# Second product of an MLP on one core: matrix rows change at a time of their own for each product, operands loaded a unit ahead in three buffers, sums on DVE

## The chip, the core and the metric

The kernel runs on one core of a Trainium2 chip. The time is that of the whole program on the device, in microseconds (us). Engines are named as in the profile: PE is TensorE (PEld its weight loads), DVE is VectorE, ACT is ScalarE, POOL is GpSimd, SP is the engine whose queue issues the DMAs.

## What is computed

A diffusion block in fp32: adaLN modulation, a mixer (a Hyena long convolution beside gated linear attention), and an MLP with a squared ReLU. The change lies in the MLP; the mixer, which takes the first half of the time, is untouched.

```python
x  = x + g1 * (mixer(...) @ w_out)
h2 = rms_norm(x, norm_mlp) * (1 + sc2) + sh2          # (2048, 1024)
x  = x + g2 * (square(relu(h2 @ w_mlp1)) @ w_mlp2)    # w_mlp1 (1024, 4096), w_mlp2 (4096, 1024)
return rms_norm(x, norm_final)
```

## The kernel before

**Arithmetic.** Every fp32 matrix product is made of three matmuls: an operand is split into a high part (a cast to fp32r by ACT, line 231 or 1570) and a low part (the rest, by DVE at 232, or by POOL at 1571), and hi x hi, hi x lo and lo x hi are summed in PSUM. On top of that both products of the MLP use a scheme of seven block products in place of eight for a 2 x 2 block product: sums and differences of blocks of either operand are formed ahead, seven products numbered 1 to 7 are taken in the order 1, 2, 6, 5, 7, 4, 3 (`ORDER`), and their results go into the four output blocks. `PR` says which combination of either operand a product reads.

**First product** (lines 1465 to 1547). For two halves of the rows (`tb`), 16 units; each holds seven products of twelve matmuls (four slices `kp`, three each, line 1374). `fill_split` makes the seven combinations of the moving operand resident in `bh`, `bl` for each `kp`; `put` squares the results and stores the seven combinations that the second product needs in DRAM, in `d_m`, by `store`. Products 4 and 3 of a unit (`late4`, `late3`) are issued within the next unit.

**Second product** (lines 1554 to 1677). 64 units: `at = 8 g + t`, t one of eight blocks of 256 output rows, g one of eight pairs of 256-row slices of `w_mlp2` (`kb` = 0, 1). A unit's product is six matmuls (`full2`: two `kb`, three each) into one PSUM bank of 128 x 512, and `more` (line 1600) adds that bank by DVE to the output block `acc` in SBUF; seven sums a unit. The PSUM bank of a unit goes on collecting, so the next product on it waits until the sum before has read it.

**What has to be ready for a unit.** (a) The operand `ur`, seven combinations of 128 x 256, loaded from `d_m` by SP (`load_u`, line 1565, two DMAs), in two buffers; per product ACT makes `uh` and POOL `ul` (`split_u`), in one tile each, so that ACT waits for the product that reads the old one. (b) The matrix rows: `w2_raw` loads a 1 MB row slice, POOL multiplies it by the gate `g2b` (four operations, line 1449) and makes two differences (1452, 1453); `w2_split` makes `wh` and `wl` for a product, and `sum_b` on POOL (1245, 1247) two more differences. Of the two `kb` slices one is replaced every four units: both `kb` have a period of eight units, four apart, for all products at the same unit boundary:

```python
    def rows(at):
        return 2 * (at // 8), 2 * ((at + 4) // 8 % 8) + 1
```

The refill of a product is issued right behind that product of the unit before (4 and 3: within the unit itself), so five splits of a change fall into one unit and two into the next. The gates of a slice are issued in two lots of two, half-way through a unit.

**Order.** Each engine, and the DMA queue of SP, works in the order of issue; what waits holds up all behind it on the same engine. Every tile is released to its next use by semaphores; the order above is written by hand.

**Ends.** `acc` is 16 tiles in a pool of its own, loaded from `d_x1` in the first eight units just before use. In the last eight units, ACT squares the block of the unit before (`squares`), POOL makes the reciprocal root, and DVE scales a row tile of 128 x 1024 (`finish`, line 1624), which SP stores.

Of the kernel before, what the change touches and what calls it, by code (L numbers as in the profile page):

```python
# [210 lines left out]
def hybrid_block(ctx: ExitStack, tc, a, out, dbg=None):  # L211
# [18 lines left out]
    def split(hi, lo, src):  # L230
        nc.scalar.copy(hi, src)  # L231
        dve.tensor_sub(lo, src, hi.bitcast(F32))  # L232
# [15 lines left out]
    d_g2 = dr.tile([P, D], F32, name="d_g2")  # L248
# [969 lines left out]
    e2 = ctx.enter_context(ExitStack())  # L1218
    bp = [sb("bp0", stack=e2), bq, bq]
# [28 lines left out]

    def fill_split(kp, r):
        pool = bp[kp]  # L1250
        hi = pool.tile([P, 7, 512], F32R, tag=f"bh{kp}", bufs=1, name="bh")
        lo = pool.tile([P, 7, 512], F32R, tag=f"bl{kp}", bufs=1, name="bl")
        for m in ORDER:
            j = PR[m][1]
            split(hi[:, j, :], lo[:, j, :], r[:, PLACE[j], :])
            sum_b(r, m, dve)
        bops[kp] = (hi, lo)
# [20 lines left out]
    with ExitStack() as eo:  # L1278
# [80 lines left out]
        ew.close()  # L1359
    e3 = ctx.enter_context(ExitStack())  # L1360
# [5 lines left out]
    g2b = us.tile([P, D], F32, name="g2b")  # L1366

    def prod(ps, w, m, kp, start, stop):
        hi, lo = w[m]
        bh, bl = bops[kp]  # L1370
        j = PR[m][1]
        sl = slice(kp * P, (kp + 1) * P)
        for i, (x_, y_) in enumerate(((hi, bh), (hi, bl), (lo, bh))):
            mm(ps[:], x_[:, sl], y_[:, j, :], start=start and i == 0, stop=stop and i == 2, skip_group_check=True)  # L1374

    def full(ps, w, m, start):
        for kp in range(4):
            prod(ps, w, m, kp, start and kp == 0, kp == 3)
# [8 lines left out]
    def put(n, tb, i, j, src, add=None):  # L1387

        tag, bufs = ("c0", 2) if i == j == 0 else ("c1", 2) if i == j else ("c", 5)
        c = us.tile([P, 512], F32, tag=tag, bufs=bufs, name="c")  # L1390
        if add is None:
            act(c[:], src[:], AF.Relu)
        else:
            dve.tensor_add(c[:], src[:], add[:])
            act(c[:], c[:], AF.Relu)
        act(c[:], c[:], AF.Square)
        cs_[n, i, j] = c
        if (i, j) != (0, 1):
# [5 lines left out]
        eng.tensor_tensor(s1[:], c[:], cs_[n, 1, 1][:], op=ALU.add)  # L1404
        eng.tensor_sub(s2[:], s1[:], cs_[n, 0, 0][:])
        dve.tensor_sub(c[:], cs_[n, 0, 0][:], c[:])
        dve.tensor_sub(s4[:], cs_[n, 1, 0][:], s2[:])
        for slot, t in ((3, c), (4, s1), (5, s2), (6, s4)):
            store(n, tb, slot, t)

    def store(n, tb, slot, c):
        step = lambda: dma(d_m[tb, n, :, :, slot, :], c[:].rearrange("p (q t) -> p q t", q=4))
        if held is None:
            step()
        else:
            held.append(step)
# [26 lines left out]
    def w2_raw(n):  # L1443

        r = w2r[n] = raw_tile()
        dma(r[:, 0:4, :], a["w2"][n])
        yield
        for q in range(4):
            gps.tensor_mul(r[:, q, :], r[:, q, :], g2b[:, (q // 2) * 512:(q // 2 + 1) * 512])  # L1449
            if q == 1:  # L1450
                yield
        gps.tensor_sub(r[:, 4, :], r[:, 3, :], r[:, 0, :])
        gps.tensor_sub(r[:, 3, :], r[:, 2, :], r[:, 3, :])

    def w2_split(n, m):
        kb = n % 2
        r, j, k = w2r[n], PR[m][1], PR[m][0]
        pool, th, tl = (mf, f"vh{k}", f"vl{k}") if kb else (wm, f"wh{k}", f"wl{k}")
        hi = pool.tile([P, 512], F32R, tag=th, bufs=1, name="wh")
        lo = pool.tile([P, 512], F32R, tag=tl, bufs=1, name="wl")  # L1460
        split(hi[:], lo[:], r[:, PLACE[j], :])
        sum_b(r, m, gps)
        w2s[m, kb] = (hi, lo)
# [3 lines left out]
    for tb in range(2):  # L1467
# [8 lines left out]
        for at in range(1, 16):  # L1476
# [5 lines left out]
            if at < 15:  # L1482
                rn = rw[ns[at + 1]] = w_raw(ns[at + 1])
            elif tb == 0:
                raws.append(fill_raw(1, 0, gps))
            else:
                for _ in w2_raw(0):
                    pass
            if at == 2 and tb == 0:
                gate_rows(g2b, us, 24, "p1")  # L1490
                dma(d_g2[:], g2b[:])
# [5 lines left out]
            if late:  # L1497
                late[0]()
# [8 lines left out]
            if late:  # L1507
                late[1]()
            if at > 1:
                w[3] = w_split(r, 3)  # L1510
            if at == 15 and tb == 0:
                raws.append(fill_raw(1, 1, gps))
            elif at == 15:
                for _ in w2_raw(1):
                    pass
# [16 lines left out]
            def late4(n=n, x=x, w=w, tb=tb):  # L1532
                full(x, w, 4, False)
                put(n, tb, 1, 0, x)

            def late3(n=n, y=y, w=w, u2=u2, tb=tb):
                full(y, w, 3, False)
                put(n, tb, 0, 1, y, u2)
# [4 lines left out]
        if tb:  # L1543

            held = []
        late[0]()
        late[1]()
    e3.close()
    eq.close()
# [4 lines left out]
    uu = sb("uu", side="right", stack=em)  # L1554
    uts, ops = {}, {}
    NU = 64

    def rows(at):
        return 2 * (at // 8), 2 * ((at + 4) // 8 % 8) + 1

    def load_u(at):
        t = at % 8
        uts[at] = uu.tile([P, 2, 7, P], F32, tag="ur", bufs=2, name="ur")
        for kb, n in enumerate(rows(at)):
            dma(uts[at][:, kb], d_m[t // 4, n, :, t % 4])

    def split_u(at, m):
        hi, lo = (uu.tile([P, 2, P], F32R, tag=f"{t}{m}", bufs=1, name=t) for t in ("uh", "ul"))
        src = uts[at][:, :, PR[m][0], :]
        nc.scalar.copy(hi[:], src)  # L1570
        (gps if at else dve).tensor_sub(lo[:], src, hi[:].bitcast(F32))  # L1571
        ops[at, m] = (hi, lo)

    load_u(0)
    load_u(1)
    for step in held:
        step()
    e2.close()
    mf = sb("mf", stack=em)
    for m in ORDER[:5]:  # L1580
        split_u(0, m)
        w2_split(1, m)
    acc = [mf.tile([P, D], F32, name=f"acc{t}") for t in range(16)]
    nf = mf.tile([P, D], F32, name="nf")
    dma(nf[:], a["norm_final"].partition_broadcast(P))
    g2b = mf.tile([P, D], F32, name="g2b")
    dma(g2b[:], d_g2[:])
# [9 lines left out]
    def more(ps, t, i, j):  # L1597

        ac = acc[2 * t + i][:, j * 512:(j + 1) * 512]
        dve.tensor_add(ac, ac, ps[:])  # L1600
# [9 lines left out]
    def squares(t):  # L1610
        rs_ = []
        for i in range(2):
            ss = mf.tile([P, 4], F32, tag="ss", bufs=4, name="ss")
            for j in range(2):
                tmp = mf.tile([P, 512], F32, tag="tmp", bufs=4, name="tmp")
                act(tmp[:], acc[2 * t + i][:, j * 512:(j + 1) * 512], AF.Square, accum_out=ss[:, j:j + 1])
            gps.tensor_add(ss[:, 2:3], ss[:, 0:1], ss[:, 1:2])
            rs_.append(rstd_of(mf, ss[:, 2:3], 1, 1.0 / D, "mrs"))
        return rs_

    def finish(t, rs_):
        for i in range(2):
            x2, tile = acc[2 * t + i], 2 * t + i
            dve.scalar_tensor_tensor(x2[:], x2[:], rs_[i][:], nf[:], op0=ALU.mult, op1=ALU.mult)
            dma(out[tile * P:(tile + 1) * P, :], x2[:])

    late = None
    prep = iter(())
    for at in range(NU):
        g, t = divmod(at, 8)  # L1630
        if g == 0:
            for i in range(2):
                dma(acc[2 * t + i][:], d_x1[(2 * t + i) * P:(2 * t + i + 1) * P, :])
# [10 lines left out]
        refill(at, 4)  # L1644
        full2(x, at, 6, False)
        more(x, t, 0, 1)
        refill(at + 1, 6)
        if late:
# [10 lines left out]
        refill(at + 1, 5)  # L1659
        full2(x, at, 7, False)  # L1660
        more(x, t, 1, 1)
        refill(at + 1, 7)
        if rs_:
            finish(t - 1, rs_)
# [9 lines left out]
        late = (late4, late3)  # L1674
    late[0]()
    late[1]()
    finish(7, squares(7))


# [16 lines left out]
```

## Time and profile before

| what | us |
|---|---|
| median of three runs (lowest, highest) | 2703.89 (2701.45, 2707.12) |
| the profiled execution, its own time | 2693.43 |
| its span, first to last instruction | 2691.6 |
| PE busy in the span | 2501.2 (93%) |
| DVE busy | 1573.9 (58%) |
| POOL busy | 1165.4 (43%) |
| ACT busy | 1162.6 (43%) |
| second product, first to last matmul | 1956.3 to 2681.5 |

Busy time of PE is modelled from the start and size of each matmul and overlaps with its neighbours: a matmul of 128 x 512 is shown with 0.39 us, while they start 0.23 us apart when nothing is in their way. So stalls of PE are read from the number of matmuls in a stretch of time, not from its busy share. In a row of waits the columns are the total, the number of times and the longest; in a row of the windows view, each engine has its busy time with the number of instructions in brackets, then come the granted clock of PE, the busy share of the DMA engines and what they moved in GB/s; in a row of an operation by tile, its number, its shortest, median and longest duration in ns, and the first and last start. In the timeline and in the chain, a row begins with its start and its duration.

### The profile page before, as it was taken

What the parts mean: (1) busy time and instruction counts of PE and PEld (TensorE: products, weight loads), DVE (VectorE), ACT (ScalarE), POOL (GpSimd) and SP (SyncE); (2) the same over time, 40 slices, a digit from 0 to 9 for tenths busy, and PEclk for the clock granted to TensorE, in tenths of its full rate; (3) what the DMA queues carried; (4) which work ended last, traced back from release to release, by engine and by line L of the source; (5) the groups of instructions that cost most, each with busy time, mean ns of one, the idle gap of its engine ahead of it and who ended that gap; (6) DMA issues with size and microseconds to landing.
All of it is one profiled execution on the core that took longest, in us unless ns stands there. A gap on an engine that the chain in (4) does not pass through costs nothing.

```text
span 2691.6 us, 38121 instructions
## 1 busy us (share of the span) xinstructions
PE 2501.2 (93%) x13320; PEld 2061.2 (77%) x13320; DVE 1573.9 (58%) x2530; ACT 1162.6 (43%) x2270; POOL 1165.4 (43%) x1155
## 2 busy tenths in 40 slices
PE   9798999999998789899999998999989898989887
PEld 5678978898887778688778886888867677777765
DVE  5754366735567777734555557555564555555557
ACT  6464352225225556334555555555532323232334
POOL 2130231214112223233244444444677776777677
PEclk9899999999999899899999999999999998999999
DMA  5425444433547786556445555454573333333333
GB/s 194 145 80 175 122 134 141 136 113 99 173 149 198 216 249 188 188 188 216 144 148 157 152 149 169 149 159 150 153 277 124 102 108 105 108 104 108 110 105 149
DMA packets 300143, 406.08 MB, mean 151 GB/s; under 512 B 24740, under 2 KB 224296, under 8 KB 289712
## 3 DMA queue, kind: packets, MB, share of 16 engines
q1 hardware_dynamic: 297072, 395.27, 46.5%
q10 hardware_dynamic: 2880, 8.39, 0.8%
q8 instruction: 105, 1.72, 0.3%
q14 instruction: 86, 0.70, 0.1%
HBM read 272.97 MB, written 130.62 MB: 150 GB/s over the span
## 4 chain that ended last, share of the span: by engine, by line
PE 40%; POOL 5%; DMA 5%; DVE 4%; issue 3%; ACT 2%; SPq 0%; POOLq 0%; ACTq 0%; DVEq 0%
PE ps L1374 21%; PE ps L1594 13%; DMA ur<-d_m 3%; POOL ul L1571 3%; PE po L227 2%; PE po L228 2%; PE po L226 2%; POOL raw L1449 1%; DVE wl L232 1%; DVE bl L232 1%; DMA raw<-in_w_dram 1%; DMA raw<-in_w_out_dram 1%; DVE acc L1600 1%; ACT wh L231 1%; ACT uh L1570 1%
## 5 line engine op out<-in xcount | busy, mean ns | idle before, releaser
L232 DVE TENSOR_TENSOR wl<-raw,wh 128x512 fp32r<-128x512 f32 x336 | 342.3, 1031 | 202.5 <-ACT wh L231 201.8
L1571 POOL TENSOR_TENSOR ul<-ur,uh 128x256 fp32r<-128x256 f32 x441 | 362.4, 848 | 168.8 <-ACT uh L1570 151.0
L1594 PE MATMUL ps<-wh,uh 128*128 128x512 f32 x896 | 363.2, 406 | 66.6 <-DVE acc L1600 44.0
L1600 DVE TENSOR_TENSOR acc<-acc,ps 128x512 f32<-128x512 f32 x448 | 300.5, 683 | 185.8 <-PE ps L1594 181.7
L1594 PE MATMUL ps<-wh,ul 128*128 128x512 f32 x896 | 360.5, 403 | 11.8 <-POOL ul L1571 11.5
L1594 PE MATMUL ps<-wl,uh 128*128 128x512 f32 x896 | 359.8, 402 | 0.0
L1570 ACT CAST uh<-ur 128x256 fp32r<-128x256 f32 x448 | 161.5, 403 | 453.9 <-DMA ur<-d_m 301.0
L1374 PE MATMUL ps<-bh,wh 128*128 128x512 f32 x896 | 350.6, 393 | 6.8 <-ACT bh L231 2.4
L1374 PE MATMUL ps<-bh,wl 128*128 128x512 f32 x896 | 350.4, 392 | 3.2 <-DVE wl L232 3.2
L1374 PE MATMUL ps<-bl,wh 128*128 128x512 f32 x896 | 351.0, 392 | 2.6 <-DVE bl L232 2.5
L231 ACT CAST wh<-raw 128x512 fp32r<-128x512 f32 x336 | 207.0, 620 | 207.5 <-PE ps L1374 168.2
L1594 PEld LDWEIGHTS ps<-wh,uh 128*128 128x128 f32 x896 | 175.0, 195 | 117.8 <-ACT uh L1570 57.0
L1594 PEld LDWEIGHTS ps<-wh,ul 128*128 128x128 f32 x896 | 174.5, 195 | 56.6 <-POOL ul L1571 19.2
L1374 PEld LDWEIGHTS ps<-bh,wh 128*128 128x128 f32 x896 | 169.3, 189 | 46.5 <-ACT bh L231 4.0
L1594 PEld LDWEIGHTS ps<-wl,uh 128*128 128x128 f32 x896 | 174.9, 195 | 36.3
L1374 PEld LDWEIGHTS ps<-bl,wh 128*128 128x128 f32 x896 | 169.2, 189 | 39.7 <-DVE bl L232 4.6
L1374 PEld LDWEIGHTS ps<-bh,wl 128*128 128x128 f32 x896 | 169.0, 189 | 39.0 <-DVE wl L232 4.0
L226 PE MATMUL ph<-hth,whi 128*128 128x512 f32 x384 | 150.9, 393 | 0.0
L226 PE MATMUL pv<-whi,hth 128*128 128x264 f32 x512 | 147.4, 288 | 3.2 <-ACT whi L231 2.9
L228 PE MATMUL ph<-hth,wlo 128*128 128x512 f32 x384 | 149.6, 390 | 0.4 <-DVE wlo L232 0.4
L227 PE MATMUL ph<-htl,whi 128*128 128x512 f32 x384 | 149.4, 389 | 0.0
L228 PE MATMUL pv<-whi,htl 128*128 128x264 f32 x512 | 145.5, 285 | 0.4 <-DVE htl L348 0.4
(284 smaller groups left out, 5047.9 us busy)
## 6 DMA issues: line engine op xcount, KB each, us to landing
ur<-d_m SPq DMA_DIRECT2D x128, 448.0 KB, 3.6
raw<-in_w_dram SPq DMA_DIRECT2D x48, 1024.0 KB, 6.3
d_m<-c SPq DMA_DIRECT2D x128, 256.0 KB, 2.6
d_m<-s SPq DMA_DIRECT2D x96, 256.0 KB, 3.3
xt<-in_x_dram SPq DMA_DIRECT2D x32, 512.0 KB, 4.4
mwt<-in_wada_dram SPq DMA_DIRECT2D x64, 256.0 KB, 3.0
raw<-in_wi_vg_dram SPq DMA_DIRECT2D x20, 528.0 KB, 4.7
wada<-in_wada_dram SPq DMA_DIRECT2D x16, 512.0 KB, 7.3
```

The source lines that it names most:

```text
L226: mm(ps, lh, rh, start=first, stop=False)
L227: mm(ps, lh, rl, start=False, stop=False)
L228: mm(ps, ll, rh, start=False, stop=last)
L231: nc.scalar.copy(hi, src)
L232: dve.tensor_sub(lo, src, hi.bitcast(F32))
L1374: mm(ps[:], x_[:, sl], y_[:, j, :], start=start and i == 0, stop=stop and i == 2, skip_group_check=True)
L1449: gps.tensor_mul(r[:, q, :], r[:, q, :], g2b[:, (q // 2) * 512:(q // 2 + 1) * 512])
L1570: nc.scalar.copy(hi[:], src)
L1571: (gps if at else dve).tensor_sub(lo[:], src, hi[:].bitcast(F32))
L1594: mm(ps[:], x_[:, kb, :], y_[:], start=start and kb + i == 0, stop=kb == 1 and i == 2, skip_group_check=True)
L1600: dve.tensor_add(ac, ac, ps[:])
```

## The change

- Each product has its own time for a new row slice (`CHANGE`): 1, 2 and 6 change one unit earlier than 5, 7, 4 and 3, whose change stays; `load_u` then takes two DMAs for a slice that straddles.
- `ur` has three buffers, loaded three units ahead (two before); `uh` and `ul` have two tiles for each product.
- The differences of the matrix rows (`sum_b` in the second product, and two in `w2_raw`) go from POOL to DVE. The four gates stay on POOL, issued one at a time, each between two refills (`slot`).
- In a refill the operand's copies are issued ahead of the matrix's.
- The turn: the resident operand of slices 0 and 3 is cut into tiles of 128 x 512, the last two products of the first stage read slice 0 last, their `put`s move behind the first loads and splits of the second product, and all four combinations of the last unit are made on POOL. `acc` now lies in the space of the resident operand of slices 1 and 2, loaded in pairs of tiles.
- The gate rows `g2b` stay in SBUF, where they went through DRAM.
- Squares and the final scaling are cut into halves of a row tile, the scaling issued one half at a time between products; of the last block, three of four squares are issued ahead of the last product. The guard `at + 4 < NU` around `w2_raw` is gone.

```diff
-    bp = [sb("bp0", stack=e2), bq, bq]
+    bp = [sb("bp0", stack=em), bq, bq]
...
+    def part(kp, h, j):
+        return bp[kp].tile([P, 512], F32R, tag=f"b{h}{kp}_{j}", bufs=1, name=f"b{h}")
...
+    g2b = sb("gp", stack=em).tile([P, D], F32, name="g2b")
...
-        eng = dve if tb and n < 1 else gps
-        eng.tensor_tensor(s1[:], c[:], cs_[n, 1, 1][:], op=ALU.add)
-        eng.tensor_sub(s2[:], s1[:], cs_[n, 0, 0][:])
-        dve.tensor_sub(c[:], cs_[n, 0, 0][:], c[:])
-        dve.tensor_sub(s4[:], cs_[n, 1, 0][:], s2[:])
+        eng = dve if held is None else gps
+        gps.tensor_tensor(s1[:], c[:], cs_[n, 1, 1][:], op=ALU.add)
+        gps.tensor_sub(s2[:], s1[:], cs_[n, 0, 0][:])
+        eng.tensor_sub(c[:], cs_[n, 0, 0][:], c[:])
+        eng.tensor_sub(s4[:], cs_[n, 1, 0][:], s2[:])
...
-    def w2_raw(n):
+    def w2_raw(n, engs):
 
         r = w2r[n] = raw_tile()
         dma(r[:, 0:4, :], a["w2"][n])
-        yield
-        for q in range(4):
-            gps.tensor_mul(r[:, q, :], r[:, q, :], g2b[:, (q // 2) * 512:(q // 2 + 1) * 512])
-            if q == 1:
-                yield
-        gps.tensor_sub(r[:, 4, :], r[:, 3, :], r[:, 0, :])
-        gps.tensor_sub(r[:, 3, :], r[:, 2, :], r[:, 3, :])
+
+        def gate(q):
+            engs[q].tensor_mul(r[:, q, :], r[:, q, :], g2b[:, (q // 2) * 512:(q // 2 + 1) * 512])
+
+        return [*(lambda q=q: gate(q) for q in range(4)),
+                lambda: dve.tensor_sub(r[:, 4, :], r[:, 3, :], r[:, 0, :]),
+                lambda: dve.tensor_sub(r[:, 3, :], r[:, 2, :], r[:, 3, :])]
...
-        sum_b(r, m, gps)
-        w2s[m, kb] = (hi, lo)
+        sum_b(r, m, dve)
+        w2s[m, n % 2] = (hi, lo)
...
+    for step in more_w2:
+        step()
+
+    puts = [f((1, 2, 3, 0)) for f in late]
     e3.close()
-    eq.close()
...
-    def rows(at):
-        return 2 * (at // 8), 2 * ((at + 4) // 8 % 8) + 1
+    CHANGE = {(m, kb): (7, 3)[kb] if m in (1, 2, 6) else (8, 4)[kb] for m in ORDER for kb in range(2)}
+
+    def row(at, m, kb):
+        return 2 * ((at + 8 - CHANGE[m, kb]) // 8 % 8) + kb
...
-        uts[at] = uu.tile([P, 2, 7, P], F32, tag="ur", bufs=2, name="ur")
-        for kb, n in enumerate(rows(at)):
-            dma(uts[at][:, kb], d_m[t // 4, n, :, t % 4])
+        uts[at] = uu[0].tile([P, 2, 7, P], F32, tag="ur", bufs=3, name="ur")
+        for kb in range(2):
+            n, n_ = row(at, 1, kb), row(at, 5, kb)
+            if n == n_:
+                dma(uts[at][:, kb], d_m[t // 4, n, :, t % 4])
+            else:
+                dma(uts[at][:, kb, 0:3], d_m[t // 4, n, :, t % 4, 0:3])
+                dma(uts[at][:, kb, 3:7], d_m[t // 4, n_, :, t % 4, 3:7])
...
+    def u_tile(at, h, m):
+        return uu[(h, m) not in U0 or at % 2].tile([P, 2, P], F32R, tag=f"u{h}{m}{at % 2}", bufs=1, name=f"u{h}")
...
     load_u(0)
     load_u(1)
...
+    load_acc(0)
+    for m in (1, 2, 6):
+        w2_split(1, m)
+        split_u(0, m)
+    for m in (5, 7):
+        w2_split(1, m)
+    load_u(2)
+    load_acc(1)
+    held = []
+    for f in puts:
+        f()
     for step in held:
         step()
...
         if at < NU:
-            for kb, n in enumerate(rows(at)):
-                if at % 8 == 4 * kb or at == 0:
+            split_u(at, m)
+            for kb in range(2):
+                n = row(at, m, kb)
+                if n != row(at - 1, m, kb) if at else m in (4, 3):
                     w2_split(n, m)
-            split_u(at, m)
...
+    def slot():
+
+        for todo in (prep, ends):
+            if todo:
+                todo.pop(0)()
...
     for at in range(NU):
         g, t = divmod(at, 8)
-        if g == 0:
-            for i in range(2):
-                dma(acc[2 * t + i][:], d_x1[(2 * t + i) * P:(2 * t + i + 1) * P, :])
+        prep, coming = prep + coming, []
         x, y = pt(), pt()
         full2(x, at, 1, True)
         more(x, t, 0, 0)
         refill(at + 1, 1)
+        slot()
...
         refill(at, 3)
-        if at + 2 < NU:
-            load_u(at + 2)
-        if at % 4 == 0 and at + 4 < NU:
-            prep = w2_raw(rows(at + 4)[at // 4 % 2 ^ 1])
-        next(prep, None)
-        rs_ = squares(t - 1) if g == 7 and t else None
+        slot()
+        if g == 0 and t < 6:
+            load_acc(t + 2)
+        if at + 3 < NU:
+            load_u(at + 3)
+        if at % 4 == 0:
+            coming = w2_raw(row(at + 4, 1, 1 - at // 4 % 2), [gps] * 4)
...
+            for i in range(2):
+                rs = scale_of(t - 1, i)
+                ends.extend(lambda i=i, j=j, rs=rs, t=t: finish(t - 1, i, j, rs) for j in range(2))
```

More of the change, by code (lines that the diff above doesn't have):

```diff
@@ L1373, in prod, with full @@
         for i, (x_, y_) in enumerate(((hi, bh), (hi, bl), (lo, bh))):
[L1374 to L1378, printed above, removed]
+            mm(ps[:], x_[:, sl], y_[j], start=start and i == 0, stop=stop and i == 2, skip_group_check=True)
+    def full(ps, w, m, start, kps=(0, 1, 2, 3)):
+        for kp in kps:
+            prod(ps, w, m, kp, start and kp == kps[0], kp == kps[3])
     def keep(ps, tag):
@@ L1411, in store @@
     def store(n, tb, slot, c):
-        step = lambda: dma(d_m[tb, n, :, :, slot, :], c[:].rearrange("p (q t) -> p q t", q=4))
+        at = [PR[m][0] for m in ORDER].index(slot)
+        step = lambda: dma(d_m[tb, n, :, :, at, :], c[:].rearrange("p (q t) -> p q t", q=4))
         if held is None:
@@ L1486, in hybrid_block @@
             else:
-                for _ in w2_raw(0):
-                    pass
+                for step in w2_raw(0, [gps] * 4):
+                    step()
             if at == 2 and tb == 0:
                 gate_rows(g2b, us, 24, "p1")
-                dma(d_g2[:], g2b[:])
             full(x, w, 1, True)
@@ L1497, in hybrid_block @@
             if late:
-                late[0]()
+                late[0]()()
             if at > 1:
@@ L1507, in hybrid_block @@
             if late:
-                late[1]()
+                late[1]()()
             if at > 1:
@@ L1575, in hybrid_block, with load_acc, acc @@
     load_u(1)
+    first_u.update({(h, m): u_tile(0, h, m) for h, m in U0})
+    acc4 = {}
+    def load_acc(t):
+        if t % 2 == 0:
+            acc4[t // 2] = bq.tile([P, 4, D], F32, tag=("bh1", "bl1", "bh2", "bl2")[t // 2], bufs=1, name="acc")
+        v = acc4[t // 2][:, 2 * (t % 2):2 * (t % 2) + 2, :]
+        dma(v, d_x1[2 * t * P:2 * (t + 1) * P, :].rearrange("(i p) d -> p i d", i=2))
+    def acc(t, i, j):
+        return acc4[t // 2][:, 2 * (t % 2) + i, j * 512:(j + 1) * 512]
+    load_acc(0)
[9 more added lines that the diff above has]
+        f()
     for step in held:
@@ L1579, in hybrid_block @@
     mf = sb("mf", stack=em)
-    for m in ORDER[:5]:
+    uu.append(mf)
+    for m in (5, 7):
         split_u(0, m)
[L1582 to L1587, printed above, removed]
     def full2(ps, at, m, start):
@@ L1610, in squares @@
-    def squares(t):
-        rs_ = []
-        for i in range(2):
[L1613 to L1625, printed above, removed]
+    def square(t, i, j):
+        if (t, i) not in sums:
+            sums[t, i] = mf.tile([P, 4], F32, tag="ss", bufs=4, name="ss")
+        tmp = mf.tile([P, 512], F32, tag="tmp", bufs=1, name="tmp")
+        act(tmp[:], acc(t, i, j), AF.Square, accum_out=sums[t, i][:, j:j + 1])
@@ new lines, in scale_of, with finish @@
+    def scale_of(t, i):
+        ss = sums.pop((t, i))
+        gps.tensor_add(ss[:, 2:3], ss[:, 0:1], ss[:, 1:2])
+        return rstd_of(mf, ss[:, 2:3], 1, 1.0 / D, "mrs")
+    def finish(t, i, j, rs):
+        v, tile = acc(t, i, j), 2 * t + i
+        dve.scalar_tensor_tensor(v, v, rs[:], nf[:, j * 512:(j + 1) * 512], op0=ALU.mult, op1=ALU.mult)
+        dma(out[tile * P:(tile + 1) * P, j * 512:(j + 1) * 512], v)
+    def slot():
+        for todo in (prep, ends):
+            if todo:
+                todo.pop(0)()
@@ L1627, in hybrid_block @@
+    sums, prep, ends = {}, [], []
     late = None
-    prep = iter(())
+    coming = []
     for at in range(NU):
         g, t = divmod(at, 8)
-        if g == 0:
-            for i in range(2):
-                dma(acc[2 * t + i][:], d_x1[(2 * t + i) * P:(2 * t + i + 1) * P, :])
+        prep, coming = prep + coming, []
         x, y = pt(), pt()
@@ L1674, in hybrid_block @@
         late = (late4, late3)
+    while ends:
+        slot()
+    square(7, 0, 0)
+    square(7, 1, 1)
     late[0]()
+    square(7, 1, 0)
+    r1 = scale_of(7, 1)
     late[1]()
-    finish(7, squares(7))
+    square(7, 0, 1)
+    r0 = scale_of(7, 0)
+    for i, rs in ((1, r1), (0, r0)):
+        for j in range(2):
+            finish(7, i, j, rs)
 def kernel(**inputs):
```

76 lines of the change are left out of this document (46 added, 30 removed).

## The prediction

> **What bounds the kernel now.** The page comes first: its busy shares and the chain that ended last.
>
> ```profile
> PE 2501.2 (93%) x13320; PEld 2061.2 (77%) x13320; DVE 1573.9 (58%) x2530; ACT 1162.6 (43%) x2270; POOL 1165.4 (43%) x1155
> PE 40%; POOL 5%; DMA 5%; DVE 4%; issue 3%; ACT 2%; SPq 0%; POOLq 0%; ACTq 0%; DVEq 0%
> ```
>
> TensorE is the engine to feed, but the shares are averages over stages. So the windows view comes next: a stretch inside the first product of the MLP, then the second product cut in three (units 0 to 7, 8 to 55, 56 to 63), and the chain in order of time for the price of one matmul.
>
> ```profile
> 1375.00:1575.00 200.00, 200.00 (x884) 165.62 (x883) 109.55 (x127) 110.40 (x188) 92.39 (x63) 1.00 0.51 154
> 1951.20:2051.20 100.00, 82.77 (x335) 64.84 (x335) 60.58 (x87) 33.15 (x83) 76.10 (x79) 0.95 0.62 223
> 2051.20:2588.10 536.90, 485.94 (x2019) 389.54 (x2019) 298.46 (x421) 162.91 (x420) 393.73 (x431) 0.96 0.31 106
> 2588.10:2681.50 93.40, 83.20 (x338) 65.22 (x336) 63.92 (x79) 41.62 (x118) 68.64 (x97) 0.95 0.40 143
> 1362.32 264.36 PE ps L1374 x1166
> 1950.82 0.39 PE L1374 MATMUL ps<-bh,wl 128*128 128x512 f32 x1
> L1594 PE MATMUL ps<-wh,ul x896: 387/389/632, 1957.4 to 2681.1; 128*128 128x512 f32 x180
> ```
>
> In the first product TensorE never rests: 264.36 us / 1166 = 0.2267 us a matmul, at a granted clock of 1.00. The second product has the same matmuls, 3 x 896 = 2688, worth 609.4 us. It takes from 1951.2 (1950.82 + 0.39) to 2681.5: 730.3 us. So some 121 us are stall, and the three windows give it away by 0.2267 a matmul: 100.0 - 335 x 0.2267 = 24 us at the start, 536.9 - 2019 x 0.2267 = 79 us in the middle, 93.4 - 338 x 0.2267 = 17 us in the last eight units. Nothing else in the kernel is worth looking at for this change.
>
> Now the waits in the middle stretch, the DMA queue's own wait there, one piece of the chain, and one DVE row from a unit that runs clean.
>
> ```profile
> ACT uh L1570 <- DMA ur<-d_m: 251.5, 44, 10.5
> DVE wl L232 <- ACT wh L231: 91.8, 30, 5.7
> PEld ps L1594 <- ACT uh L1570: 33.6, 13, 4.3
> PE ps L1594 <- DVE acc L1600: 28.8, 14, 3.9
> PEld ps L1594 <- ACT wh L231: 20.0, 9, 4.1
> PE ps L1594 <- ACT wh L231: 15.9, 6, 3.7
> SPq L1565 <- POOL ul L1571: 566.9, 56, 15.0
> 2181.02 2.99 POOL ul L1571 x3
> 2184.39 4.15 DMA ur<-d_m
> 2192.37 1.20 POOL ul L1571
> 2193.95 4.59 DMA ur<-d_m
> 2203.24 3.75 POOL raw L1449 x3
> 2062.32 0.69 DVE L1600 TENSOR_TENSOR acc<-acc,ps 128x512 f32<-128x512 f32 x1 [0.67 <-PE ps L1594]
> ```
>
> The loop is: POOL makes the last low part of a unit, that frees one of two `ur` buffers, SP issues the next load (it waited 566.9 us for POOL), the load lands, ACT copies, POOL subtracts, TensorE starts. When POOL is late, the load is late, and ACT stands at a landing (251.5 us) with the matrix copies `wh` queued behind it; DVE stands at `wh` (91.8 us) with its sums into `acc` queued behind that, and TensorE at both. POOL is late because at each change of matrix rows it also has four gates, four differences (1452, 1453, 1245, 1247) and five refills together. In the clean unit a sum comes every 0.69 + 0.67 = 1.36 us, a product of six matmuls; seven make a unit of 9.52 us.
>
> **The change, part by part.** Durations of the pieces:
>
> ```profile
> L232 DVE TENSOR_TENSOR wl<-raw,wh x112: 677/868/1808, 1958.7 to 2644.4; 128x512 fp32r<-128x512 f32 x112
> L1449 POOL TENSOR_TENSOR raw<-raw,g2b x60: 1279/1294/1311, 1972.5 to 2564.9; 128x512 f32<-128x512 f32 x60
> L1245 POOL TENSOR_TENSOR raw<-raw x16: 1264/1284/1662, 1959.4 to 2628.7; 128x512 f32<-128x512 f32 x16
> L1571 POOL TENSOR_TENSOR ul<-ur,uh x441: 717/738/1710, 1962.8 to 2675.5; 128x256 fp32r<-128x256 f32 x147
> L1600 DVE TENSOR_TENSOR acc<-acc,ps x448: 672/686/691, 1968.7 to 2682.0; 128x512 f32<-128x512 f32 x150
> L1570 ACT CAST uh<-ur x448: 388/403/412, 1955.9 to 2675.0; 128x256 fp32r<-128x256 f32 x150
> L231 ACT CAST wh<-raw x112: 601/617/628, 1958.0 to 2643.8; 128x512 fp32r<-128x512 f32 x112
> DMA to landing us min/median/max: 6.3/7.1/7.9
> DMA to landing us min/median/max: 3.3/3.6/5.6
> ```
>
> (The two landings are those of the 1 MB `raw` rows and of the 448 KB halves of `ur`.)
>
> 1. Three `ur` buffers and two sets of operand tiles. The load is issued half-way through unit at for unit at+3, whose copies begin with unit at+2: one and a half units, 14 us, against two halves of at most 5.6. The ACT wait goes, and with it the chain piece POOL, DMA, ACT. ACT and POOL may run a unit (9.52 us) ahead. What is late next is a matrix row, not an operand.
>
> 2. Sums and differences from POOL to DVE: four per change. POOL loses 4 x 1.28 = 5.1 us and keeps, over four units, 28 x 0.738 + 4 x 1.294 = 25.8 of 38.1 us. DVE gets 4 more two-input operations. No row shows these on DVE; the nearest is `wl`, the same shape from the same tile: 0.68 alone, 0.87 median, 1.81 at worst. I take 0.87 and keep 0.68 and 1.81. Over four units DVE then has 28 x 0.686 + 11 x 0.87 = 28.8 of 38.1. Both fit, so what counts is where they cluster.
>
> 3. Rows change for products 1, 2, 6 one unit earlier than for 5, 7, 4, 3, spread over three units as 3, 2, 2 splits. The thickest is the first: 7 sums, 3 `wl` and 2 differences, 4.8 + 5 x 0.87 = 9.2 us of DVE against 9.52. From the end of product 1: a sum to 0.69, `wl` and a difference to 2.43, a sum, `wl` and a difference to 4.86, and after two more sums, at 6.2 us, product 7 may overwrite what the second of them read; it is due at 5 x 1.36 = 6.8. No stall at 0.87; at 1.81 that sum ends at 4 x 0.69 + 4 x 1.81 = 10.0, so 3.2 us a change. I take 0.8 a change as the nearer end: 15 changes, 12 us (0 to 48).
>
> 4. The gates are dropped singly between refills and DVE's two differences queue behind the fourth, with all DVE sums behind them. The unit has 4 gates and 4 refills to get through: 5.2 + 3.0 = 8.2 us from the landing. Rows are asked for half a unit before that unit, after the two `ur` halves: some 7.1 + 3.6 = 10.7 us later they are there, 6 us into the unit at the latest if POOL was in step, and DVE reaches the difference 7.5 us in. But POOL is ahead: it frees `ur` up to a unit earlier, so the rows land before the unit starts and the gates end at about 5. Taken at nothing; the cover is POOL's lead, and without it the cost is 6 + 8.2 - 7.5 - 2 (the slack that TensorE has, a product and a half) = 4.7 us a change, 70 us in all.
>
> 5. ACT keeps its work (7 x 0.403 + 7/4 x 0.617 = 3.9 us a unit). Copies now stand ahead of `wh`, which still waits for TensorE to leave the old rows; that costs the lead of one product and nothing on the path.
>
> 6. The turn from the first product to the second. What TensorE does there now:
>
> ```profile
> 1951.39 4.40 DMA ur<-d_m
> 1956.33 0.80 PE L1594 MATMUL ps<-wh,uh 128*128 128x512 f32 x1 [5.12 <-ACT uh L1570]
> 1957.35 0.63 PE L1594 MATMUL ps<-wh,ul 128*128 128x512 f32 x1
> 1957.78 0.63 PE L1594 MATMUL ps<-wh,uh 128*128 128x512 f32 x1
> 1961.84 0.39 PE L1594 MATMUL ps<-wh,uh 128*128 128x512 f32 x1
> 1968.68 2.08 DVE L1600 TENSOR_TENSOR acc<-acc,ps 128x512 f32<-128x512 f32 x3 [1.89 <-DMA acc<-d_x]
> L1404 POOL TENSOR_TENSOR s<-c x2: 1291/1291/1291, 1919.4 to 1938.5; 128x512 f32<-128x512 f32 x2
> L1405 POOL TENSOR_TENSOR s<-s,c x2: 1793/1793/1793, 1920.8 to 1939.9; 128x512 f32<-128x512 f32 x2
> ```
>
> Now the first two loads can start before the last matmul, because the fourth fill of the operand is cut into tiles of its own and the last products read fill 0 last; but they stand on SP behind the stores of the last full unit, so about 2 of the 5.1 us go. After the idle time matmuls start every 0.43 us (1957.35, 1957.78), at 0.63 us each, and are back at 0.39 by 1961.84, 5.5 us on. The Trainium skill (TensorE: Matmul & The Clock Gate, What's actually happening) has the clock halved after an idle window of about 3.4 us; the rows agree, and by it a turn that idles for less would take 2 us more off: 2611. Against this, SP has about 9 MB to move in some 25 us (four unit loads, three of `acc`, one of rows, five stores), the four closing differences of the last unit now all lie on POOL (about 4 x 1.3 to 1.8 us) ahead of its first refills, and the first gates wait behind those loads. I put the start at 16 us lost (24 now), with 8 and 26 as ends.
>
> 7. Last eight units: finishing half a row at a time (1.28 us becomes two of 0.64) between products, so 17 becomes a change x 0.8, about 1 for the finishing and about 3 for a last set of rows that is loaded and gated for no unit (4 x 1.294 us on POOL, with DVE's two differences behind): 5, ends 2 and 17. After the last matmul only one square is left instead of four, and a half row leaves earlier:
>
> ```profile
> 2686.41 1.28 DVE L1624 SCALAR_TENSOR_TENSOR acc<-acc,mrs,nf 128x1024 f32<-128x1024 f32 x1 [0.99 <-POOL mrs L281]
> ```
>
> about 2 us less. The gate kept in SBUF instead of in DRAM, and tiles cut finer in the first product, touch no wait on the chain: nothing.
>
> Sum: start 24 to 16, middle 79 to 10 (12 of the 15 changes x 0.8), end 17 to 5, tail 2: 8 + 69 + 12 + 2 = 91 us. The profiled execution took 2693.43 (span 2691.6), 10.5 below the median of the runs, 2703.89; it would be 2602, the median about 2613.
>
> **The rivals.**
>
> *DVE and POOL lock each other out* at the changes. The spread of `wl` (0.68 to 1.81) speaks for it, and of `ul` (0.72 to 1.71); sums that read `ps` do not suffer (0.672 to 0.691). If each of the five operations waits out one `ul`, it takes 0.68 + 0.74 = 1.42, the sum ahead of product 7 ends at 2.8 + 4 x 1.42 = 8.5, 1.7 after it is due, and the unit has 4.8 + 7.1 = 11.9 us of DVE: 2.4 over. 15 x 2.4 = 36 instead of 12: 2637. Against it: POOL is busy only two thirds of the time. The Trainium skill (SBUF — State Buffer, Who interferes with whom) says that an operation of DVE with two SBUF inputs and a GpSimd one that reads SBUF exclude each other for the whole instruction; the rows above agree, and by it the move of sums to DVE is no free one.
>
> *The gates come late* (step 4): 70 us back, 2683. For: SP serves one queue. Against: POOL's slack of 12 us in four units. If only half of it comes back, 2648.
>
> *The change does not do it*: SP still issues late because other loads stand in front, and half of the middle stays: 2613 + 35 = 2648, or with all of it no change.
>
> *Slower*: the same place as step 4, with DVE blocked for longer. From 91 / 15 = 6.1 us a change on it decides: the rows then land 7.4 us into the unit (7.4 + 8.2 - 7.5 - 2 = 6.1), 12 us after they were asked for. At 10 us into it the price is 8.7 a change and the time 2613 + 130 = 2743. The landings of at most 7.9 for a quiet queue speak against it.
>
> **How the numbers follow.** Chances: forecast 0.62, lock 0.17, late gates 0.09, no effect or half of it 0.06, slower 0.06. The time is the forecast's, 2613. The low end takes every unknown at its good end: start 8, no stall at changes, end 2, so 8 + 10 + 3 = 21 us less, 2592. The high end takes in the lock and half of the late gates: 2658. Less than 0.2% (5.4 us) no comparison of this kernel can tell from nothing; the three runs lie within 5.7. Faster 0.91, same 0.03, slower 0.06.
>
> **What would show it.** Right: the second product takes 640 us or less, nearly all units at 9.52; ACT's wait for `ur` is gone; POOL's busy time there falls by 80 us and DVE's rises by 50 to 60. Wrong: TensorE waiting on DVE's sums in the unit of the 3 splits (the lock), DVE waiting for the gates with TensorE behind it (step 4), ACT still at landings (no effect), or a granted clock below 1.00 in long clean stretches, which would make the matmul itself dearer.

## The result, and the profile after

The median goes from 2703.89 us to 2683.73 us (2669.51 to 2691.03, nine runs each): a ratio of 0.9923, 95% interval 0.9904 to 0.9943. The change is worth 20 us; the forecast was 91. The profiled execution took 2681.11 (span 2679.3).

The page of the changed kernel, its busy shares:

```profile
PE 2497.2 (93%) x13320; PEld 2068.7 (77%) x13320; DVE 1613.7 (60%) x2619; ACT 1186.3 (44%) x2273; POOL 1077.1 (40%) x1093
```

Against the page before it shows 88 us less of POOL and 40 us more of DVE, and nothing of where the time went. The windows tell more. The first row is a clean stretch of the first product, the next three are the second product cut at the same units as before (0 to 7, 8 to 55, 56 to 63), the last the whole of it:

```profile
1375.00:1575.00 200.00, 200.00 (x884) 165.62 (x883) 109.96 (x127) 111.75 (x189) 92.73 (x64) 1.00 0.51 154
1959.30:2063.80 104.50, 84.39 (x335) 67.23 (x335) 61.01 (x91) 35.90 (x87) 71.07 (x78) 0.90 0.64 234
2063.80:2578.90 515.10, 476.89 (x2018) 389.34 (x2017) 317.38 (x469) 180.91 (x420) 331.89 (x385) 0.96 0.33 111
2578.90:2669.90 91.00, 82.71 (x340) 64.13 (x338) 72.06 (x103) 42.87 (x115) 60.73 (x90) 0.96 0.36 129
1959.30:2669.90 710.60, 643.99 (x2689) 520.71 (x2688) 450.45 (x661) 259.68 (x622) 463.70 (x551) 0.95 0.38 131
```

The second product takes 710.6 us where it took 730.3. Against clean units of 9.52 us (8, 48 and 8 of them) the start loses 28 us (24 before), the middle 58 (80 before) and the end 15 (17 before). The first product ends at 1959.3, 8.1 us later than before; 6.3 us of that are there when it starts (1317.7 against 1311.4), behind the untouched mixer. In the profiles of this study it ends anywhere from 1951 to 1969, so below the second product is compared by its own length.

The waits of the middle stretch:

```profile
ACT uh L1597 <- PE ps L1640: 308.9, 286, 6.3
DVE raw L1464 <- POOL raw L1461: 58.1, 12, 6.2
PEld ps L1640 <- DVE acc L1645: 43.3, 12, 4.9
PE ps L1640 <- DVE acc L1645: 38.2, 12, 4.5
DVE wl L232 <- ACT wh L231: 11.7, 18, 0.7
POOL raw L1461 <- DMA raw<-in_w_dram: 10.1, 9, 2.1
```

The row that led before, ACT at a landing of `ur` (251.5 us), is gone: ACT now waits for TensorE alone. `wl` behind `wh` fell from 91.8 to 11.7. What took their place is a single wait, 12 times in the 12 changes of this stretch: DVE stands 58.1 us at the first of the two differences (line 1464), because POOL is not through with the gates (1461), and TensorE stands behind DVE's sums. The chain through one change holds, between TensorE's matmuls, only POOL's last refill and gate, the difference and DVE's sums behind it:

```profile
2215.35 38.40 PE ps L1640 x162
2253.75 0.03 POOLq L1598
2253.78 0.20 POOL ul L1598
2253.98 1.26 POOL raw L1461
2255.23 0.02 issue
2255.26 1.20 DVE raw L1464
2256.46 0.60 DVE acc L1645
...
2257.58 0.68 DVE acc L1645
```

And the same change on the timeline, first POOL, then DVE, then TensorE, whose last two rows are the first and the last of eight slow matmuls:

```profile
2248.80 1.28 POOL L1461 TENSOR_TENSOR raw<-raw,g2b 128x512 f32<-128x512 f32 x1 [0.78 <-DMA raw<-in_w_dram]
...
2250.74 2.54 POOL L1461 TENSOR_TENSOR raw<-raw,g2b 128x512 f32<-128x512 f32 x2
...
2253.94 1.28 POOL L1461 TENSOR_TENSOR raw<-raw,g2b 128x512 f32<-128x512 f32 x1
...
2249.69 0.69 DVE L1645 TENSOR_TENSOR acc<-acc,ps 128x512 f32<-128x512 f32 x1 [0.67 <-PE ps L1640]
2255.26 1.20 DVE L1464 TENSOR_TENSOR raw<-raw 128x512 f32<-128x512 f32 x1 [4.88 <-POOL raw L1461]
...
2254.71 0.39 PE L1640 MATMUL ps<-bh,ul 128*128 128x512 f32 x1
2258.31 0.50 PE L1640 MATMUL ps<-wh,uh 128*128 128x512 f32 x1 [3.22 <-DVE acc L1645]
...
2259.35 0.63 PE L1640 MATMUL ps<-bl,uh 128*128 128x512 f32 x1
...
2262.33 0.58 PE L1640 MATMUL ps<-bh,ul 128*128 128x512 f32 x1
```

POOL has the rows 0.78 us after it wants them and gates them in 6.4 us (2248.80 to 2253.94 + 1.28), four gates and two refills. DVE comes to the difference right behind the first gate (2249.69 + 0.69), waits 4.88 us for the fourth, and its sums wait with it. TensorE idles 3.22 us; behind four matmuls at nearly the old pace, eight start 0.43 us apart instead of 0.2267, 1.6 us more. That makes 4.8 us, which is also the mean of the 12 changes (58 / 12). They are not alike: TensorE idles 2.2 to 4.5 us, 38.2 in all. The three shortest idle times (2.2 to 2.3 us) are followed by no slow matmul, the nine from 2.5 us on by 6 to 13 of them, for 2.7 to 5.7 us.

By the Trainium skill (TensorE: Matmul & The Clock Gate, What's actually happening) an idle window of about 3.4 us halves the clock and a busy one of that length gives it back. The slow stretch shown, 3.4 us, agrees; the idle time before it is shorter than that window, as in five of the nine, and here the measured times decide.

### The profile page after: what moved, and what is told of

Same layout as the page of the kernel before. It is cut to its first block, busy times and chain, and to the rows that moved or that the text cites. A ratio compares the mean times of both kernels' runs of the same rounds, so it can differ in the third digit from the quotient of the medians.

```text
span 2679.3 us, 38019 instructions
## 1 busy us (share of the span) xinstructions
PE 2497.2 (93%) x13320; PEld 2068.7 (77%) x13320; DVE 1613.7 (60%) x2619; ACT 1186.3 (44%) x2273; POOL 1077.1 (40%) x1093
## 5 line engine op out<-in xcount | busy, mean ns | idle before, releaser
L1597 ACT CAST uh<-ur 128x256 fp32r<-128x256 f32 x448 | 179.8, 406 | 408.8 <-PE ps L1640 387.5
L232 DVE TENSOR_TENSOR wl<-raw,wh 128x512 fp32r<-128x512 f32 x276 | 266.7, 978 | 97.0 <-ACT wh L231 94.2
L231 ACT CAST wh<-raw 128x512 fp32r<-128x512 f32 x276 | 170.6, 622 | 201.8 <-PE ps L1384 165.5
L1640 PE MATMUL ps<-wh,uh 128*128 128x512 f32 x448 | 183.5, 410 | 66.4 <-DVE acc L1645 58.2
L1640 PE MATMUL ps<-wh,ul 128*128 128x512 f32 x448 | 179.4, 400 | 0.3 <-DVE ul L1598 0.2
L1640 PE MATMUL ps<-bh,uh 128*128 128x512 f32 x448 | 179.5, 401 | 0.0
L1640 PE MATMUL ps<-bl,uh 128*128 128x512 f32 x448 | 179.5, 401 | 0.0
L1640 PE MATMUL ps<-wl,uh 128*128 128x512 f32 x448 | 179.2, 400 | 0.0
L1640 PE MATMUL ps<-bh,ul 128*128 128x512 f32 x448 | 179.0, 400 | 0.0
L1640 PEld LDWEIGHTS ps<-wh,uh 128*128 128x128 f32 x448 | 87.8, 196 | 96.0 <-DVE acc L1645 63.3
```

Source lines behind the costliest of these rows:

```text
L1640: mm(ps[:], x_[:, kb, :], y_[:], start=start and kb + i == 0, stop=kb == 1 and i == 2, skip_group_check=True)
```

## The experiments

The question was why DVE waits at a change: because the rows or their gates are late (step 4 as the forecast has it), or because the differences stand too early in DVE's queue; and then what each other part is worth. A clean unit is 9.52 us, the whole product 609.4. All lengths below are of the second product, from the last matmul of the first, in the one profiled execution of each kernel; "lost" is at the start, in the middle and at the end. Each ratio is to runs of the kernel before the change beside it.

| kernel | median us | ratio, 95% interval | second product | lost |
|---|---|---|---|---|
| before | 2703.9 | 1 | 730.3 | 24, 80, 17 |
| after | 2683.7 | 0.9923, 0.9904 to 0.9943 | 710.6 | 28, 58, 15 |
| differences in place (e3_diffs_late) | 2615.8 | 0.9691, 0.9665 to 0.9718 | 641.7 | 15, 0, 17 |
| differences on POOL (e2_diffs_pool) | 2623.5 | 0.9712, 0.9681 to 0.9743 | 648.1 | 14, 6, 18 |
| one boundary (s2_one_boundary) | 2620.0 | 0.9701, 0.9674 to 0.9729 | 640.3 | 16, 0, 15 |
| all sums on POOL (s3_sums_pool) | 2693.1 | 0.9982, 0.9966 to 0.9998 | 719.1 | 28, 64, 17 |
| the same, in place (s5_sums_pool_in_place) | 2654.2 | 0.9804, 0.9751 to 0.9858 | 676.8 | 25, 23, 20 |
| two `ur` buffers (s1_two_buffers) | 2718.8 | 1.0064, 1.0047 to 1.0081 | 746.0 | 22, 94, 20 |
| the same, single operands (s1b_single_operands) | 2700.6 | 0.9994, 0.9979 to 1.0010 | 727.1 | 18, 81, 20 |
| scaling in place (f1_finish_in_place) | 2610.0 | 0.9665, 0.9645 to 0.9684 | 638.9 | 15, 0, 15 |
| scaling later (f2_finish_later) | 2613.2 | 0.9662, 0.9636 to 0.9687 | 632.4 | 15, 1, 8 |

**Where the two differences stand in DVE's queue.** The text issues the four gates and the two differences in successive slots, and the splits of that slice a unit later. The built program keeps the slot within the unit, but not the unit. The text asks for rows in units 0, 4, 8, 12 and so on to 60; in the trace of the changed kernel the sixteen loads (line 1458) go out in units 0, 3, 5, 8, 12 and so on to 56, the last at 2585.8 us. So from the fourth on, loads, gates and differences stand a whole change ahead of the text. Among the instructions that DVE runs, the two differences of the third slice are numbers 2019 and 2021 (2040.48 and 2042.20 us) and the first split that reads the slice is number 2063 (2088.33 us): 44 instructions, more than four units, later. So the result for which DVE stops is not needed for four units. By what rule the builder moves them no run here shows. The edit keeps those two at their place in the text, and nothing else:

```diff
-                lambda: dve.tensor_sub(r[:, 4, :], r[:, 3, :], r[:, 0, :]),
-                lambda: dve.tensor_sub(r[:, 3, :], r[:, 2, :], r[:, 3, :])]
+                lambda: tc.keep_in_program_order(dve.tensor_sub(r[:, 4, :], r[:, 3, :], r[:, 0, :])),
+                lambda: tc.keep_in_program_order(dve.tensor_sub(r[:, 3, :], r[:, 2, :], r[:, 3, :]))]
```

> The changed kernel, with the two differences of a row slice held at their place in the text: on DVE they stand right ahead of the splits that read them, where in the changed kernel they stand some 44 instructions (four units) ahead of them. Nothing else moves by hand. Queue theory (DVE stands at gates that nobody needs yet, 4.9 us in each of 15 changes): the wait goes and with it some 60 us, 2620 (2605 to 2635). Late-rows theory (rows and gates are late for the splits themselves): the wait moves to the splits, 2684 within 10. Lock theory (two-input work on DVE and POOL's work exclude each other): as many operations on both, 2684 within 10.

2615.84 us: 68.9 us off the second product. POOL and SP run the same instructions in the same order as in the changed kernel, and ACT all but two; on DVE the differences of a slice come a change later. Its windows (start, middle, end):

```profile
1959.40:2050.60 91.20, 81.83 (x339) 65.67 (x340) 64.91 (x86) 34.37 (x86) 72.39 (x79) 0.94 0.72 266
2050.60:2508.00 457.40, 456.89 (x2014) 377.18 (x2013) 328.03 (x468) 180.35 (x419) 344.90 (x383) 1.00 0.36 124
2508.00:2601.10 93.10, 81.66 (x339) 63.39 (x337) 75.18 (x104) 42.51 (x115) 61.23 (x90) 0.98 0.35 126
```

Its waits in the middle, those that answer to the rows above:

```profile
ACT uh L1597 <- PE ps L1640: 241.2, 270, 1.5
...
POOL raw L1461 <- DMA raw<-in_w_dram: 12.1, 10, 3.3
```

A change on the timeline, DVE and then POOL:

```profile
2217.43 1.19 DVE L1464 TENSOR_TENSOR raw<-raw 128x512 f32<-128x512 f32 x1
...
2221.69 1.05 DVE L232 TENSOR_TENSOR bl<-raw,bh 128x512 fp32r<-128x512 f32 x1
...
2216.08 1.29 POOL L1461 TENSOR_TENSOR raw<-raw,g2b 128x512 f32<-128x512 f32 x1 [0.93 <-DMA raw<-in_w_dram]
...
2218.03 3.46 POOL L1461 TENSOR_TENSOR raw<-raw,g2b 128x512 f32<-128x512 f32 x2
...
2222.13 1.76 POOL L1461 TENSOR_TENSOR raw<-raw,g2b 128x512 f32<-128x512 f32 x1
```

The middle runs at the clean pace, 457.4 for 48 x 9.52 = 457.0, at a granted clock of 1.00; no wait of DVE for a gate is left in it. The rows come no earlier (POOL still waits 12.1 us for landings, 10.1 before). The timeline shows what is gone: the difference at 2217.43 runs before POOL has made the second to fourth gates, so it reads the slice gated a change earlier, and the first split comes 4.3 us behind it. No wait moved to the splits, so for them rows and gates are not late, and with as many operations on both engines the lock theory has no part in it: it is the place in DVE's queue. What it rests on is that rows and gates still stand a change ahead; a kernel with these in place too was not run.

**The same two on POOL.** There only refills would stand behind them.

```diff
+                lambda: gps.tensor_sub(r[:, 4, :], r[:, 3, :], r[:, 0, :]),
+                lambda: gps.tensor_sub(r[:, 3, :], r[:, 2, :], r[:, 3, :])]
```

> The changed kernel with the two differences of a row slice back on POOL, behind its four gates; the two further differences of a split stay on DVE. Queue theory: DVE no longer stands at the gates, 2620 to 2635 (POOL has 2.6 us more per four units and 12 to spare). Late-rows theory: the first split's difference on DVE waits for POOL instead, 2675 to 2690. Lock theory: 30 of 62 operations go, at most 0.4 us each: 2672.

2623.49: nearly the same gain by another way. POOL can afford 2.6 us a change; 6 us of the middle are its price.

**Spreading the change over three units (step 3).** On top of the kernel with differences in place, all products change at one unit again:

```diff
-    CHANGE = {(m, kb): (7, 3)[kb] if m in (1, 2, 6) else (8, 4)[kb] for m in ORDER for kb in range(2)}
+    CHANGE = {(m, kb): (8, 4)[kb] for m in ORDER for kb in range(2)}
```

> As the one with late differences, but the rows change for all seven products at one unit boundary (five splits in one unit, two in the next). From the step for the thickest unit: 5 splits, 2 differences and 7 sums are 4.8 + 7 x 0.87 = 10.9 us of DVE against 9.52, so 1.4 to 3 us a change, 20 to 45 us above the one with late differences. If spreading is worth nothing, the same within 6.

2619.95, the second product 640.3 against 641.7, the middle clean. The spread is worth nothing here: once DVE does not stand at the gates, five splits in one unit do not hold TensorE up.

**All four differences on POOL, as before the change.** What remains of the change is the third buffer, the second set of operand tiles, the spread and the ends.

```diff
+                lambda: gps.tensor_sub(r[:, 4, :], r[:, 3, :], r[:, 0, :]),
+                lambda: gps.tensor_sub(r[:, 3, :], r[:, 2, :], r[:, 3, :])]
...
-        sum_b(r, m, dve)
+        sum_b(r, m, gps)
```

> The changed kernel with all four differences of a change back on POOL: the part 'sums on DVE' undone, the rest kept. Queue theory: no wait of DVE for the gates, but POOL's differences sit between its refills and each split waits for them: 2625 to 2645. Lock theory: the best of the three, below the one with late differences. If the sums on DVE were the gain of this change: 2690 or more.

2693.1: I had expected little of the other two sums, and missed. They are worth 719.1 - 648.1 = 71 us. Waits of its middle:

```profile
PE ps L1640 <- DVE acc L1645: 45.9, 12, 5.6
ACT wh L231 <- POOL raw L1243: 33.3, 6, 6.3
ACT bh L231 <- POOL raw L1243: 28.6, 6, 5.3
```

Line 1243 is the sum that stands between the first split of a slice and the others. ACT waits for it up to 6.3 us at every change, DVE's `wl` waits for ACT, the sums for `wl`, TensorE for the sums. To tell POOL's load from the place in its queue, the same with all four kept where the text has them:

```diff
-            eng.tensor_sub(r[:, 0, :], r[:, 2, :], r[:, 4, :])
+            o = eng.tensor_sub(r[:, 0, :], r[:, 2, :], r[:, 4, :])
...
+        if eng is gps:
+            tc.keep_in_program_order(o)
```

> As s3_sums_pool (all four differences of a slice on POOL, 2693 us), each now kept at its place in the text in POOL's queue. Theory A (their place in POOL's queue was at fault in s3, as it was in DVE's in the changed kernel): 2620 to 2645. Theory B (POOL itself is the wrong place for the two sums that stand between splits, since the copies and splits of the same slice wait for them and POOL's refills, which wait for TensorE's progress, stand ahead of them in any order): 2675 to 2700, units 2 and 6 of each eight long as in s3.

676.8, between the two theories: by this profile 42 us of the 71 were place, and 29 remain for having the sums on POOL. The middle alone loses 23 us, and `wh` still waits up to 3.7 us for the sum. The split is rough, since the four runs of this kernel lie between 2640 and 2665 us; that the 29 come from refills that stand ahead and wait for TensorE is argued, not shown.

**The third buffer (step 1).** Differences in place, but loads two units ahead in two buffers; then also `uh` and `ul` in one tile each:

```diff
-        uts[at] = uu[0].tile([P, 2, 7, P], F32, tag="ur", bufs=3, name="ur")
+        uts[at] = uu[0].tile([P, 2, 7, P], F32, tag="ur", bufs=2, name="ur")
...
-    load_u(2)
...
-        if at + 3 < NU:
-            load_u(at + 3)
+        if at + 2 < NU:
+            load_u(at + 2)
```

> The kernel with the two differences kept in place (2616 us, second product 641.7), with the third ur buffer taken away: loads go out two units ahead, as before the change; operand tiles stay doubled. Theory (the lateness of POOL was the cause of the late loads, and the four differences taken from POOL removed it): a load still lands within half a unit of its request, nothing waits, 2612 to 2625. Rival (step 1 as predicted: the third buffer is what takes ACT's wait for ur away): the wait for landings is back at the changes, 2 to 4 us each, 2645 to 2675.

> As s1_two_buffers, and uh and ul again in one tile for each product, as before the change. Theory (lead over several units is not needed once POOL has 5 us less to do at a change): within 10 us of s1_two_buffers, 2612 to 2635. Rival (the lead of a unit carries ACT and POOL over the changes): a split of a product then starts only behind the product before, four gates and four refills of POOL come between, TensorE waits 2 to 4 us at each change for ul, 2645 to 2675.

2718.78 and 2700.55: my theory that POOL's relief alone had cured the late loads is false, and the forecast's own step 1 is right; the rival's range, 2645 to 2675, was too low as well. Waits of the middle with two buffers, of the engines and of SP's queue:

```profile
ACT uh L1597 <- DMA ur<-d_m: 229.1, 44, 9.0
SPq L1582 <- POOL ul L1598: 443.5, 42, 16.3
```

Two loads in a row on its timeline:

```profile
2147.32 1.64 ACT L1597 CAST uh<-ur 128x256 fp32r<-128x256 f32 x5 [7.91 <-DMA ur<-d_m]
2147.80 5.88 POOL L1598 TENSOR_TENSOR ul<-ur,uh 128x256 fp32r<-128x256 f32 x7 [5.36 <-ACT uh L1597]
...
2152.31 9.83 SPq L1582 DMA_DIRECT2D ur<-d_m  x3
...
2156.91 0.71 ACT L1597 CAST uh<-ur 128x256 fp32r<-128x256 f32 x2 [6.30 <-DMA ur<-d_m]
```

The old row is back, 229.1 us in 44 waits (251.5 in 44 before the change): landing, ACT's copies, POOL's seven refills, the next request, the next landing 4.6 us after it. With two buffers the request comes when POOL gives a buffer back, and that load is wanted at once; the third takes a unit out of that loop and is worth 746.0 - 641.7 = 104 us. The second set of operand tiles is worth nothing without it (746.0 against 727.1 with one set); with three buffers it was not taken away.

**The end.** With the differences in place, unit 58 takes 17.6 us, and DVE's final scaling (line 1669) waits there for POOL's reciprocal root. That wait in the last units:

```profile
DVE acc L1669 <- POOL mrs L280: 9.8, 8, 5.4
```

The scaling was first kept at its place in the text, then issued three slots later as well:

```diff
+        tc.keep_in_program_order(dve.scalar_tensor_tensor(v, v, rs[:], nf[:, j * 512:(j + 1) * 512], op0=ALU.mult, op1=ALU.mult))
...
+            ends.extend([lambda: None] * 3)
             for i in range(2):
                 rs = scale_of(t - 1, i)
```

> The kernel with the two differences kept in place, and the final scaling of half rows (L1669) kept at its place in the text too. Theory (the loss of some 16 us in units 57 to 59 is the same fault as that of the changes: the scaling stands too early in DVE's queue, behind a reciprocal root that POOL has not made, and the sums stand behind it): about 6 to 12 us less, 2604 to 2610. Rival (POOL is what is late there, with four gates, refills and roots in one queue, and any place soon after waits): no change, 2613 to 2619.

> As f1_finish_in_place, with each scaling issued three slots (three products, about 4 us) later. Theory (queue place): at least as good as f1, all but 2 to 4 us of the 16 gone, 2600 to 2607. Rival (POOL late by more than 5 us): as f1 or between, 2608 to 2616. A later scaling adds nothing at the end if the last unit's own scaling is what ends the kernel.

In place the second product is 2.8 us shorter (638.9), and DVE still waits 9.3 us for the root: POOL is late with it. Three slots later the product is 9.3 us shorter, 632.4, and the wait 4.7 us. The last eight units of the second kernel:

```profile
2517.70:2601.60 83.90, 79.35 (x339) 62.47 (x337) 72.74 (x102) 43.06 (x115) 63.34 (x90) 1.00 0.39 136
```

83.9 against 93.1. The medians of the two (2609.97 and 2613.22) do not show it, and fall one into its theory's range and one into its rival's: in the profile of the second kernel the first product ended 11.5 us later (1969.2 against 1957.7). Both are the best versions found, some 90 us below the kernel before and 70 below the changed one.

## Why the prediction was wrong

**What held.** The bound (stalls of the second product, 121 us) and the loop through POOL, load and ACT were right. Step 1: ACT's wait for `ur` is gone from the middle, and its third buffer is what removes it. Step 2: POOL's busy time in the second product fell from 538.5 us (the sum of its three windows) to 463.7, by 75 where 80 was said; DVE's rose by 27.5 where 50 to 60 was said, since `wl` became shorter. With the place of two instructions mended, the kernel loses 15, 0 and 17 us where the forecast had 16, 10 and 5, and takes 2615.84 us where it had 2613. The start was priced rightly; that the sums agree is luck, for the middle was priced 10 us too high and the end 12 too low.

**The step that failed is step 4**: gates dropped singly, the two differences queued behind the fourth, "Taken at nothing; the cover is POOL's lead". The lead brings no row earlier. The rows were to be asked for half a unit before their unit and to land before it starts, and the gates to end at about 5 us. In the change shown above the unit starts at 2242.69 (its first matmul), and this stands ahead of it, a refill of POOL and two rows of SP:

```profile
2240.50 0.94 POOL L1598 TENSOR_TENSOR ul<-ur,uh 128x256 fp32r<-128x256 f32 x1 [0.64 <-ACT uh L1597]
...
2241.47 0.80 SPq L1582 DMA_DIRECT2D ur<-d_m  x2
2242.31 0.43 SPq L1458 DMA_DIRECT2D raw<-in_w_dram  x1
```

The rows are asked for 0.4 us before the unit, behind a load of `ur` that goes out as the refill ends at 2241.44. The refills come one a product, each behind a copy of ACT, and ACT waits for TensorE (308.9 us in 286 waits): read so, POOL gives a buffer back when TensorE lets it, whatever lead it has. (In six of the 12 changes SP then waits another 0.3 us for DVE before it asks for the rows; what would hold that load next was not tried.) Over the 12 changes the first gate starts 5.7 to 7.4 us into the unit and the fourth ends 11.5 to 13.8 us in, while DVE reaches the difference 7.7 us in each time, as the step had it (7.5). So the case without cover is the one that came.

The step's price for that case, 4.7 us a change and 70 us in all, and the rival's 2683 are what came (4.8 a change, 68.9 us, 2683.73), and the wait is the one they describe. That they agree so closely is luck: the first gate starts 6.4 us in on average (6 taken for the rows), gates and refills take 6.1 (8.2 taken), TensorE has 1.7 of slack (2 taken), and the slowed matmuls add 1.6 that the price did not have.

What neither the step nor its rival had is that DVE stops for a result that nothing reads for four units. The forecast read the order from the text, and the section on the kernel's order says the same; that is true only of instructions for which the builder is told so. With the differences in place the gates end later still (12.9 to 16.8 us into the unit) and cost nothing. The trace before the change has such a lead too: the last of its fifteen loads goes out at 2552.3 us, near the start of unit 53, where the text has unit 56.

**Step 3** was a mis-sized term: 12 us in all (0 to 48), and the thick unit cost nothing in the middle once DVE was not held. The lock rival, 36 us on the same place, falls with it. (The high end, 2658, does not follow from the prices it names: the lock's 24 us over the forecast and half of the late gates, 35, make 2672; the measured 2683.73 lies above both.) Rows by tile in the changed kernel's middle:

```profile
L232 DVE TENSOR_TENSOR wl<-raw,wh x42: 676/691/1008, 2065.9 to 2576.9; 128x512 fp32r<-128x512 f32 x42
L1464 DVE TENSOR_TENSOR raw<-raw x12: 1195/1202/1212, 2084.8 to 2557.2; 128x512 f32<-128x512 f32 x12
L1465 DVE TENSOR_TENSOR raw<-raw x12: 677/678/680, 2086.5 to 2558.9; 128x512 f32<-128x512 f32 x12
```

The two engines do hold each other up: 1.20 for the difference that starts just behind a refill (at 2255.26, the refill at 2255.18), 0.68 for the other; and with the differences in place the gates take 1.73 (3.46 / 2) instead of 1.28 beside differences of 1.19. By the Trainium skill (SBUF — State Buffer, Who interferes with whom) an operation of DVE with two SBUF inputs contends with one of GpSimd that reads SBUF; these rows agree. With the differences in place it cost the path nothing: the middle is clean. `wl` itself got shorter, 0.69 median where 0.87 was taken.

**Step 6** said a start of 16, and it was 28. Without DVE's wait it is 15, so most of the miss is step 4 again, in the changes of the first eight units. Within it one term went the other way: the idle time between the products did not shrink by 2 us, it grew from 5.1 to 7.6. The chain there:

```profile
1958.64 0.26 SPq L1611
1958.96 0.48 SPq L1582
1959.49 6.90 DMA ur<-d_m
1966.47 0.41 ACT uh L1597
```

The first load begins 0.2 us after the last matmul, as before, and not ahead of it. It now stands behind a load of `acc` (line 1611) that the text puts after it, and lands in 6.90 us where it took 4.40. The order alone does not make it late: with the differences in place SP has the same order, the first load begins at 1958.28, 1.1 us before the last matmul, and the idle time is 5.6. In the other kernels of the table it is 5.5 to 8 us; what moves it was not tried.

**Step 7** said an end of 5 and a tail 2 us shorter: 15, and 0.7. The four halves of a scaling wait for POOL's root; a later place takes the end to 8.

## What to carry to other kernels

An engine works its queue in order, so an instruction that is placed early costs whatever it waits for, however late its result is wanted: for each wait that ends on an engine of the critical path, ask what is the first reader, and look for it in the queue as built, not in the text. Before the lead of an engine is counted as cover, ask what that engine waits for itself, and which request its lead would bring forward. A forecast of moved work should be made on the built order of instructions where one can have it, and say so where one cannot. And parts that each remove one wait of a chain show little alone: here the third buffer, the sums on DVE and the place of two differences were worth 104, 71 and 69 us, each taken away with the others there (the second with the two differences on POOL), and all three are wanted for the whole.

## What was not expected of the hardware

Short stalls of TensorE were dearer here than they look: an idle time of 3.22 us cost 4.8, because matmuls behind it ran at half pace. Nine of the twelve stalls did this, the shortest with 2.5 us of idle time; three of 2.2 to 2.3 us did not. The stretch of 515 us that holds them shows a granted clock of 0.96, the same units without them 1.00. Busy time hides it: PE shows 477 us busy there, with 2018 matmuls that need 457.
